# Mixer B: turning the probabilities on VectorE instead of TensorE, with the values' steps in a new order

## The chip, the cores and the metric

The kernel runs on one core of one Trainium2 chip. The metric is the device time of one execution in microseconds (us); times given for several runs are their median. One execution was also taken by the hardware profiler, and the lines quoted below are from it.

## What is computed

The program is a two-layer encoder trunk on 256 positions of width 2048, in float32. Layer 0 uses attention mixer A, layer 1 uses mixer B; each is followed by a gated MLP. The change lies in mixer B. For each of three head groups (dilations 1, 4, 16) with eight heads of 128, the reference computes

```python
logits = einsum('bnqchd,bnkchd->bnchqk', qb, kb) * scale + bias
p = exp(logits - max(logits))
o = einsum('bnchqk,bnkchd->bnqchd', p, vb)
```

and then joins the groups with weights taken from their softmax denominators. The kernel keeps the probabilities as queries on partitions by keys on columns, and the second product needs them with keys on partitions. So every block of probabilities has to be turned once. Group 0 has 256 x 256 probabilities per head; groups 1 and 2 are computed as two diagonal blocks of 128 x 128 per head.

## The kernel before, in words

**The weight stream.** Nearly all time goes into products of activations with weight matrices that are read from memory once. A weight tile of 128 x 1024 floats is loaded by SP (`raw`), and split in two parts so that TensorE can multiply it fast and still exactly: ScalarE writes the rounded part `wh` (line 128), VectorE the rest `wl = raw - wh` (line 129). TensorE then runs 12 matmuls of 512 columns on that pair, here called a **block**: for each of two rows of weights and two halves of the positions `wh` (line 153), `wl` (154) and `wh` again with the activations' low part (155). There are six `raw` buffers and three pairs of `wh` and `wl` (NHL = 3, line 23), handed out in turn (`new_hl`, line 120). So the `wh` of a block can be written only when TensorE has finished the block three places earlier. A projection (`project`, line 180) is 8 blocks, and after each block `step()` (line 90) advances one generator: the pending small work is written into the program between the blocks of the next projection.

**Mixer B** (line 917) runs in two halves of four heads (`hf`). Each half makes, for the groups 0, 1, 2, the projections k and q with the generators `k_gen` and `s_gen`, and then three projections for the values with `v_gen` (line 1002). `s_gen` leaves the probabilities of head i in tiles `pr`: for group 0 one 128 x 256 tile for each half m of the queries, for the groups 1 and 2 one 128 x 256 tile that holds both 128 x 128 blocks. It ends (lines 991 to 1000) with the factors `e`, by which the groups are joined.

**The values before.** `v_gen` first takes the projection's result out of PSUM (`evac_split`, line 689). Then, one head per step, VectorE multiplies `pr` by its factor (line 1014), TensorE transposes the blocks of 128 x 128 into PSUM (line 1016), and ScalarE and VectorE copy the result back to SBUF as `pT`: for group 0 split into a high and a low part (lines 290, 291), for the groups 1 and 2 as one plain copy by either engine in turn (lines 78 and 80). One step later TensorE multiplies `pT` with the values: for group 0 six matmuls of 256 columns (lines 307 to 309), otherwise two of 128 columns in full float32 (line 305, two records each in the trace), and the result is split into a slot `ah`, `al` that the output projection reads.

**The other way to turn.** Keys, queries and the MLP are turned without TensorE already: VectorE's transpose turns each 32 x 32 block of a tile in place (`turn_blocks`, line 332), and `place_blocks` (line 338) moves the blocks to where they belong with 16 copies on 32 partitions each. A four-letter table says which engine takes a copy; "paaa" is 4 for GpSimd (line 345) and 12 for ScalarE (line 347).

**The order.** A scheduler of the tile framework puts the instructions of each engine into a fixed queue, and each engine works its queue strictly from the front, waiting where an input is not ready. The splits of the weights are asked for with a raised priority (AHEAD = 45).

## Time and profile before

| | |
|---|---|
| three runs | 2264.11, 2264.49, 2266.11 us; median 2264.49 |
| the profiled execution | 2266.43 us, its span 2264.6 us |
| granted TensorE clock | 0.999 of full speed |
| busy share of the span | TensorE 99%, its weight loads 82%, VectorE 73%, ScalarE 67%, GpSimd 11% |
| line 1016, the transposes in question | 64 matmuls, mean 272 ns of one |
| window from 1146.60 to 1214.45 us: values of the first half | TensorE 67.74, VectorE 40.65, ScalarE 32.02, GpSimd 0.75 us busy of 67.85 |

The span is the time from the first to the last instruction. The duration of a matmul in a row is its whole passage through the engine; matmuls overlap, so what one adds to the stream is the distance from its start to the next start.

### The profile page before, as it was taken

How to read it: one execution, taken by the hardware profiler on the slowest of the kernel's cores; microseconds unless marked ns; L12 is line 12 of the kernel's file. 1: busy time of each engine (PE TensorE's matmuls, PEld its weight loads, DVE VectorE, ACT ScalarE, POOL GpSimd, SP SyncE). 2: the span in 40 equal slices, each digit the busy share in tenths (PEclk: the TensorE clock that was granted, in tenths of full speed). 3: DMA queues.
4: the chain of work that ended last, by engine and by line, in shares of the span. 5: the costliest groups of instructions: out<-in, count | busy, mean ns of one | idle time of the engine just before them, and what ended most of it. 6: DMA issues, size and time to landing. Idle time of an engine off the chain costs nothing.

```text
span 2264.6 us, 28910 instructions
## 1 busy us (share of the span) xinstructions
PE 2247.2 (99%) x10157; PEld 1859.7 (82%) x10157; DVE 1658.6 (73%) x2243; ACT 1511.0 (67%) x2344; POOL 257.7 (11%) x372
## 2 busy tenths in 40 slices
PE   9999999999999999999999999999999999999998
PEld 7788888888888888888888888888888888888886
DVE  6776687888878788856565556465888888688895
ACT  6665776777547777767755775565777754577763
POOL 2210112200001010121100100000101100001101
PEclk9999999999999999999999999999999999999999
DMA  8444557755665655666655564565656656556664
GB/s 299 156 149 150 197 196 224 223 188 190 209 205 187 201 189 188 208 218 203 192 172 178 177 193 160 183 195 187 196 192 194 204 186 212 188 191 193 218 202 135
DMA packets 126450, 437.43 MB, mean 193 GB/s; under 512 B 17264, under 2 KB 18032, under 8 KB 126304
## 3 DMA queue, kind: packets, MB, share of 16 engines
q1 hardware_dynamic: 119744, 425.64, 57.5%
q0 software_dynamic: 6128, 9.38, 1.6%
q8 instruction: 79, 1.29, 0.2%
q14 instruction: 67, 0.55, 0.1%
q10 hardware_dynamic: 432, 0.56, 0.1%
HBM read 429.20 MB, written 6.29 MB: 192 GB/s over the span
## 4 chain that ended last, share of the span: by engine, by line
PE 80%; DVE 1%; DMA 1%; ACT 1%; issue 1%; POOL 0%; POOLq 0%; DVEq 0%; ACTq 0%
PE acc L154 21%; PE acc L155 21%; PE acc L153 21%; PE acc L273 5%; PE acc L275 5%; PE acc L278 5%; DMA scr<-lnt 1%; PE ps L305 1%; DVE wl L129 1%; ACT tM L347 0%; PE ps L1016 0%; DMA raw<-in_w_down_dram 0%; ACT wh L128 0%; PE ps L308 0%; PE ps L309 0%
## 5 line engine op out<-in xcount | busy, mean ns | idle before, releaser
L129 DVE TENSOR_TENSOR wl<-raw,wh 128x1024 fp32r<-128x1024 f32 x828 | 1017.7, 1235 | 452.7 <-ACT wh L128 449.8
L128 ACT ACTIVATE wh<-raw 128x1024 fp32r<-128x1024 f32 x828 | 872.9, 1058 | 538.0 <-PE acc L155 325.8
L153 PE MATMUL acc<-wh,xh 128*128 128x512 f32 x2176 | 852.2, 392 | 0.2 <-ACT wh L164 0.2
L154 PE MATMUL acc<-wl,xh 128*128 128x512 f32 x2176 | 848.3, 390 | 3.1 <-DVE wl L129 2.9
L155 PE MATMUL acc<-wh,xh 128*128 128x512 f32 x2176 | 847.4, 389 | 0.0
L154 PEld LDWEIGHTS acc<-wl,xh 128*128 128x128 f32 x2176 | 408.7, 188 | 89.7 <-DVE wl L129 6.3
L155 PEld LDWEIGHTS acc<-wh,xh 128*128 128x128 f32 x2176 | 408.4, 188 | 84.9
L153 PEld LDWEIGHTS acc<-wh,xh 128*128 128x128 f32 x2176 | 408.9, 188 | 83.7 <-ACT wh L164 0.7
L345 POOL COPY u<-t 32x256 f32<-32x256 f32 x176 | 110.7, 629 | 1040.3 <-DVE t L455 1032.2
L273 PE MATMUL acc<-wh,ah 128*128 128x512 f32 x520 | 202.5, 389 | 1.3 <-DVE h L408 1.3
L275 PE MATMUL acc<-wh,al 128*128 128x512 f32 x520 | 202.3, 389 | 0.0
L154 PE MATMUL acc<-wl,ah 128*128 128x512 f32 x480 | 187.1, 390 | 1.0 <-DVE wl L129 1.0
L153 PE MATMUL acc<-wh,ah 128*128 128x512 f32 x480 | 187.3, 391 | 0.1
L155 PE MATMUL acc<-wh,al 128*128 128x512 f32 x480 | 186.6, 389 | 0.0
L347 ACT ACTIVATE u<-t 32x256 f32<-32x256 f32 x352 | 147.8, 420 | 13.8 <-DVE t L455 5.8
L278 PE MATMUL acc<-wl,ah 128*128 128x512 f32 x520 | 146.1, 389 | 0.0
L273 PEld LDWEIGHTS acc<-wh,ah 128*128 128x128 f32 x520 | 97.6, 188 | 22.2 <-DVE h L408 2.0
L278 PEld LDWEIGHTS acc<-wl,ah 128*128 128x128 f32 x520 | 97.6, 188 | 20.3
L275 PEld LDWEIGHTS acc<-wh,al 128*128 128x128 f32 x520 | 97.6, 188 | 20.2
L154 PEld LDWEIGHTS acc<-wl,ah 128*128 128x128 f32 x480 | 90.1, 188 | 20.1 <-DVE wl L129 1.8
L153 PEld LDWEIGHTS acc<-wh,ah 128*128 128x128 f32 x480 | 90.1, 188 | 19.0 <-DVE cu L628 0.6
L155 PEld LDWEIGHTS acc<-wh,al 128*128 128x128 f32 x480 | 90.1, 188 | 18.5
(180 smaller groups left out, 1666.4 us busy)
## 6 DMA issues: line engine op xcount, KB each, us to landing
raw<-in_w_up_dram SPq DMA_DIRECT2D x352, 512.0 KB, 4.3
raw<-in_w_down_dram SPq DMA_DIRECT2D x176, 512.0 KB, 4.8
raw<-in_w_b_dram SPq DMA_DIRECT2D x144, 512.0 KB, 4.3
raw<-in_w_bo_dram SPq DMA_DIRECT2D x48, 512.0 KB, 4.1
raw<-in_w_a_dram SPq DMA_DIRECT2D x40, 512.0 KB, 4.5
raw<-in_w_ao_dram SPq DMA_DIRECT2D x32, 512.0 KB, 3.8
raw<-in_w_a_dram SPq DMA_DIRECT2D x16, 256.0 KB, 6.5
h<-in_x_dram SPq DMA_DIRECT2D x4, 512.0 KB, 8.2
```

Of the source, the lines that this page charges most:

```text
L128: nc.scalar.activation(wh, r, AF.Copy)
L129: nc.vector.tensor_tensor(wl, r, wh.bitcast(F32), ALU.subtract)
L153: nc.tensor.matmul(accs[m], xh, wh[:, j, :], start=st, stop=False)
L154: nc.tensor.matmul(accs[m], xh, wl[:, j, :], start=False, stop=False)
L155: nc.tensor.matmul(accs[m], xl, wh[:, j, :], start=False, stop=sp)
L273: nc.tensor.matmul(acc[k], xh, wh[:, j, :], start=k in fresh, stop=False)
L275: nc.tensor.matmul(acc[k], xl, wh[:, j, :], start=False, stop=False)
L278: nc.tensor.matmul(acc[k], xh, wl[:, j, :], start=False, stop=last[k] == i and j == 1)
L305: nc.tensor.matmul(o, lh[ls], rh[rs], start=start, stop=stop)
L345: nc.gpsimd.tensor_copy(dst, src)
L347: nc.scalar.activation(dst, src, AF.Copy)
```

## The change

`v_gen` no longer uses TensorE to turn the probabilities. After the scaling, VectorE's transpose turns the 32 x 32 blocks of `pr` into a tile `tp` of 128 x 1024 (tag "stg", two buffers that the evacuated keys and queries use too), and `place_blocks(..., "paaa")` moves them into a tile `pp`, in the space of tiles that are free by then. For group 0 one `tp` holds two heads, and ScalarE and VectorE then split `pp` into `pT` as before; for the groups 1 and 2 one `tp` holds all four heads and TensorE reads `pp` directly. The work is spread over the steps by a `plan`: for group 0 eight steps (turn, place and turn, place, split, then split and multiply), for the others five (turn, place, nothing, two heads' products, two heads' products). `s_gen` only gains a third view of the same `pr` tile.

```diff
@@ -980,7 +980,7 @@
                             pr = [hpool.tile([P, NT], F32, tag=f"a{c}{sl}", name=nm("pr")) for c in "hl"]
                         else:
                             pt = hpool.tile([P, NT], F32, tag=f"ah{sl}", name=nm("pr"))
-                            pr = [pt[:, :P], pt[:, P:]]
+                            pr = [pt[:, :P], pt[:, P:], pt]
                         for m in range(2):
                             c = 4 * m + i
                             nc.scalar.activation(pr[m], lg[:, m, :W], AF.Exp, bias=nmx[:, g, c:c + 1],
@@ -1001,41 +1001,60 @@
 
                 def v_gen(g, accs, hf=hf, probs=probs, e=e):
                     v = evac_split(bp, accs, rstd, g > 0)
-                    pTs = {}
-                    yield
-                    for k in range(5):
-                        yield
-                        if k < 4:
-                            i = k
+                    parts = {}
+                    n_ = 2 if g == 0 else 4
+
+                    def turn(u):
+                        t = parts["t", u] = bp.tile([P, 2, 512], F32, tag="stg", name=nm("tp"), bufs=2)
+                        for i in range(u * n_, u * n_ + n_):
                             pr = probs[4 * g + i]
-                            t = ps_tile()
                             for m in range(2):
                                 c = 4 * m + i
                                 nc.vector.tensor_scalar(pr[m], pr[m], e[:, g, c:c + 1], None, op0=ALU.mult)
-                                for kt in range(2 if g == 0 else 1):
-                                    nc.tensor.transpose(t[:, kt * NT + m * P:kt * NT + (m + 1) * P],
-                                                        pr[m][:, kt * P:(kt + 1) * P], ident)
-                            pT = pTs[i] = pair_tile(bp, [P, 2 * NT], "pT", 2, g > 0)
-                            n = 2 * NT if g == 0 else NT
-                            split(pT[0][:, :n], pT[1] if pT[1] is None else pT[1][:, :n], t[:, :n])
-                        if k >= 1:
-                            i = k - 1
-                            j = i % 2
-                            pT = pTs.pop(i)
-                            if j == 0:
-                                o = ps_tile()
-                            for kt in range(2):
-                                vs = (allp, kt, slice(i * P, (i + 1) * P))
                                 if g == 0:
-                                    mm3(o[:, j * NT:(j + 1) * NT], v, pT, vs,
-                                        (allp, slice(kt * NT, (kt + 1) * NT)), kt == 0, kt == 1)
-                                else:
-                                    mm3(o[:, j * NT + kt * P:j * NT + (kt + 1) * P], v, pT, vs,
-                                        (allp, slice(kt * P, (kt + 1) * P)), True, True)
-                            sl = (2 * g + hf) * 4 + i
-                            slots[sl] = new_slot(sl)
-                            hi, lo = slots[sl]
-                            split(hi, lo, o[:, j * NT:(j + 1) * NT])
+                                    nc.vector.transpose(t[:, m, i % 2 * NT:i % 2 * NT + NT], pr[m])
+                            if g > 0:
+                                nc.vector.transpose(t[:, :, i * P:(i + 1) * P],
+                                                    pr[2].rearrange("p (m c) -> p m c", m=2))
+
+                    def place(u):
+                        o = bp.tile([P, 4, NT], F32, tag=("qTl", "qTh", "kTh")[g] if u == 0 else "kTl", name=nm("pp"))
+                        place_blocks(o.rearrange("p j (m t) -> p j m t", m=2), parts.pop(("t", u)), "paaa")
+                        for i in range(n_):
+                            parts[u * n_ + i] = o[:, 2 * i:2 * i + 2, :] if g == 0 else (o[:, i, :], None)
+
+                    def low(i):
+                        src = parts[i].rearrange("p a t -> p (a t)")
+                        parts[i] = pair_tile(bp, [P, 2 * NT], "pT", 2)
+                        split(*parts[i], src)
+
+                    def value(i):
+                        j = i % 2
+                        if j == 0:
+                            parts["o"] = ps_tile()
+                        o, pT = parts["o"], parts.pop(i)
+                        for kt in range(2):
+                            vs = (allp, kt, slice(i * P, (i + 1) * P))
+                            if g == 0:
+                                mm3(o[:, j * NT:(j + 1) * NT], v, pT, vs,
+                                    (allp, slice(kt * NT, (kt + 1) * NT)), kt == 0, kt == 1)
+                            else:
+                                mm3(o[:, j * NT + kt * P:j * NT + (kt + 1) * P], v, pT, vs,
+                                    (allp, slice(kt * P, (kt + 1) * P)), True, True)
+                        sl = (2 * g + hf) * 4 + i
+                        slots[sl] = new_slot(sl)
+                        split(*slots[sl], o[:, j * NT:(j + 1) * NT])
+
+                    if g == 0:
+                        plan = ((turn, 0), (place, 0, turn, 1), (place, 1), (low, 0), (low, 1, value, 0),
+                                (low, 2, value, 1), (low, 3, value, 2), (value, 3))
+                    else:
+                        plan = ((turn, 0), (place, 0), (), (value, 0, value, 1), (value, 2, value, 3))
+                    yield
+                    for fs in plan:
+                        yield
+                        for f, a in zip(fs[::2], fs[1::2]):
+                            f(a)
 
                 for g in range(3):
                     bts = biases(hf, g)
```

The instructions stand differently in three queues. The rows below are from the first half of mixer B; the second half has the same sequence. The numbers in names tell tiles apart.

ScalarE before, from the factors `e` at the end of `s_gen` on:

```order
L995 ACTIVATE e_8857<-e_8857 128x24
L128 ACTIVATE wh_10328<-raw_10324 128x1024
L290 ACTIVATE pTh_10241<-ps_10234 128x512
L128 ACTIVATE wh_10366<-raw_10325 128x1024
L290 ACTIVATE pTh_10272<-ps_10265 128x512
L290 ACTIVATE ah_10283<-ps_10276 128x256
L128 ACTIVATE wh_10396<-raw_10392 128x1024
L290 ACTIVATE pTh_10310<-ps_10303 128x512
```

Between two weight splits there stood one or two copies. ScalarE after, from the same place on:

```order
L995 ACTIVATE e_8857<-e_8857 128x24
L128 ACTIVATE wh_10326<-raw_10322 128x1024
L128 ACTIVATE wh_10346<-raw_10323 128x1024
L347 ACTIVATE pp_10263<-tp_10234 32x8x32 x12
L347 ACTIVATE pp_10305<-tp_10280 32x8x32 x9
L128 ACTIVATE wh_10381<-raw_10377 128x1024
L347 ACTIVATE pp_10305<-tp_10280 32x8x32 x3
L290 ACTIVATE pTh_10342<-pp_10263 128x512
L128 ACTIVATE wh_10411<-raw_10378 128x1024
```

Twenty-one placing copies of the two turned tiles of group 0 now stand between `wh_10346` and `wh_10381`, the splits for two blocks that follow each other on TensorE.

VectorE before, from the first scaling on:

```order
L1014 TENSOR_SCALAR pr_9349<-pr_9349,e_8857 128x256
L1014 TENSOR_SCALAR pr_9350<-pr_9350,e_8857 128x256
L1014 TENSOR_SCALAR pr_9383<-pr_9383,e_8857 128x256
L129 TENSOR_TENSOR wl_10329<-raw_10324,wh_10328 128x1024
L291 TENSOR_TENSOR pTl_10242<-ps_10234,pTh_10241 128x512
```

VectorE after, from the same place on:

```order
L1013 TENSOR_SCALAR pr_9349<-pr_9349,e_8857 128x256
L1013 TENSOR_SCALAR pr_9350<-pr_9350,e_8857 128x256
L1015 STREAM_TRANSPOSE tp_10234<-pr_9349 128x256
L1015 STREAM_TRANSPOSE tp_10234<-pr_9350 128x256
L1013 TENSOR_SCALAR pr_9383<-pr_9383,e_8857 128x256
L1013 TENSOR_SCALAR pr_9384<-pr_9384,e_8857 128x256
L1015 STREAM_TRANSPOSE tp_10234<-pr_9383 128x256
L1015 STREAM_TRANSPOSE tp_10234<-pr_9384 128x256
L129 TENSOR_TENSOR wl_10327<-raw_10322,wh_10326 128x1024
```

Four scalings and four transposes now stand ahead of the split `wl_10327`; four more of each stand between it and `wl_10347`, and between that and `wl_10382` the four transposes of group 1 and twelve of the sixteen scalings of the groups 1 and 2. In the same way the copies of group 1 and 2 follow on ScalarE in pieces of 1, 4, 7, 4, 6 and 2 between later weight splits.

TensorE before, at the first products of group 0 (rows of the weight stream are L153 to L155):

```order
L1016 MATMUL ps_10234<-ident,pr_9349 128x128 x2
L1016 MATMUL ps_10234<-ident,pr_9350 128x128 x2
L153 MATMUL acc_10177<-wh_10249,xh_8590 128x512
L154 MATMUL acc_10177<-wl_10250,xh_8590 128x512
L155 MATMUL acc_10177<-wh_10249,xh_8590 128x512
L153 MATMUL acc_10178<-wh_10249,xh_8590 128x512
L154 MATMUL acc_10178<-wl_10250,xh_8590 128x512
L155 MATMUL acc_10178<-wh_10249,xh_8590 128x512
L1016 MATMUL ps_10265<-ident,pr_9383 128x128 x2
L307 MATMUL ps_10276<-pTh_10241,vh_10171 128x256
L308 MATMUL ps_10276<-pTl_10242,vh_10171 128x256
```

TensorE after, at the same products:

```order
L155 MATMUL acc_10178<-wh_10346,xh_8760 128x512
L153 MATMUL acc_10177<-wh_10381,xh_8905 128x512
L153 MATMUL acc_10178<-wh_10381,xh_8905 128x512
L154 MATMUL acc_10177<-wl_10382,xh_8905 128x512
L307 MATMUL ps_10366<-pTh_10342,vh_10171 128x256
L155 MATMUL acc_10177<-wh_10381,xh_8905 128x512
L154 MATMUL acc_10178<-wl_10382,xh_8905 128x512
L155 MATMUL acc_10178<-wh_10381,xh_8905 128x512
L308 MATMUL ps_10366<-pTl_10343,vh_10171 128x256
L309 MATMUL ps_10366<-pTh_10342,vl_10172 128x256
L307 MATMUL ps_10366<-pTh_10342,vh_10171 128x256
```

The transposes are gone from the queue. The first products stand inside the block of `wh_10381`, four blocks later than before, and at the head of that block two matmuls on `wh_10381` stand ahead of the first on `wl_10382`, the only place in each half where the order 153, 154, 155 is broken so.

## The prediction

> **What bounds the kernel now.** I read the page first, for the engine that is never idle, then the list of waits for what stops it.

> ```profile
> span 2264.6 us, 28910 instructions
> PE 2247.2 (99%) x10157; PEld 1859.7 (82%) x10157; DVE 1658.6 (73%) x2243; ACT 1511.0 (67%) x2344; POOL 257.7 (11%) x372
> PE 80%; DVE 1%; DMA 1%; ACT 1%; issue 1%; POOL 0%; POOLq 0%; DVEq 0%; ACTq 0%
> PE acc L154 21%; PE acc L155 21%; PE acc L153 21%; PE acc L273 5%; PE acc L275 5%; PE acc L278 5%; DMA scr<-lnt 1%; PE ps L305 1%; DVE wl L129 1%; ACT tM L347 0%; PE ps L1016 0%; DMA raw<-in_w_down_dram 0%; ACT wh L128 0%; PE ps L308 0%; PE ps L309 0%
> ```

> TensorE is busy for 99% of the span, and the chain that ended last is its weight stream. The transposes of line 1016 are in that chain too. The waits of TensorE from 900 to 1480 us, which holds all of mixer B, are one row:

> ```profile
> engine line waited for: us in total, times, longest us
> PE acc L154 <- DVE wl L129: 0.5, 1, 0.5
> ```

> So in mixer B nothing stops TensorE, and whatever leaves its queue comes off the time, unless something new makes it wait. Both sides are worked out below for one half of mixer B; the halves are alike:

> ```profile
> core 0: us, PE busy (x) PEld busy (x) DVE busy (x) ACT busy (x) POOL busy (x), PEclk, DMA share, GB/s
> 1146.60:1214.45 67.85, 67.74 (x344) 56.67 (x342) 40.65 (x73) 32.02 (x50) 0.75 (x1) 1.00 0.52 168
> 1359.81:1427.68 67.87, 67.75 (x343) 56.66 (x342) 40.66 (x73) 32.02 (x50) 0.00 (x0) 1.00 0.50 164
> ```

> Each window runs from one weight matmul behind a score product to one behind the last product of the values but one. It holds 21 blocks.

> **What the transposes cost.** The row of line 1016 gives 272 ns for each of 64, but they overlap, so I take what they add to the stream.

> ```profile
> L1016 PE MATMUL ps<-ident,pr 128*128 128x128 f32 x64 | 11.2, 272 | 0.2
> 1164.43 0.39 PE L155 MATMUL acc<-wh,xh 128*128 128x512 f32 x1
> ...
> 1165.84 0.39 PE L155 MATMUL acc<-wh,xh 128*128 128x512 f32 x1
> ...
> 1189.29 0.39 PE L155 MATMUL acc<-wh,xh 128*128 128x512 f32 x1
> 1189.52 0.60 PE L305 MATMUL ps<-pT,v 128*128 128x128 f32 x4
> ...
> 1190.42 0.39 PE L155 MATMUL acc<-wh,xh 128*128 128x512 f32 x1
> 1190.65 0.39 PE L153 MATMUL acc<-wh,xh 128*128 128x512 f32 x1
> ...
> 1193.37 0.39 PE L153 MATMUL acc<-wh,xh 128*128 128x512 f32 x1
> ```

> From 1190.65 to 1193.37 are 12 weight matmuls, so one takes 0.227 us and a block 2.72. The six products of a head of group 0 lie between the line-155 matmuls at 1164.43 and 1165.84, beside three weight steps: 1.41 - 0.68 = 0.73. The four records of line 305 in the same way: 1.13 - 0.68 = 0.45. The window holds 252 weight matmuls (57.1), four heads of group 0 (2.9) and eight of the others (3.6), together 63.6 of 67.85. The rest, **4.2 us**, is 32 transposes and the small wait ahead of the first, 0.13 us each. About 0.1 is given back, since the first head's products are now cut in two by three weight matmuls. I take 4.1 per half, 8.2 in all.

> **What is added beside the stream.** Per half ScalarE gets 48 placing copies and gives up four copies from PSUM, VectorE gets 16 transposes and gives up four copies, GpSimd gets 16 copies. With 32 and 41 us busy of 68, ScalarE and VectorE have room in the mean, and GpSimd is idle. So where the new work stands decides, and I follow one stretch.

> **The wait that is added.** ScalarE now has 21 placing copies in one piece between the weight splits `wh_10346` and `wh_10381`. Behind them wait `wh_10381`, then VectorE's `wl_10382`, then TensorE. The rows for the walk:

> ```profile
> 1149.19 0.39 PE L155 MATMUL acc<-wh,xh 128*128 128x512 f32 x1
> 1149.41 0.39 PE L153 MATMUL acc<-wh,xh 128*128 128x512 f32 x1
> 1149.66 1.06 ACT L128 ACTIVATE wh<-raw 128x1024 fp32r<-128x1024 f32 x1 [0.22 <-PE acc L155]
> 1056.57 2.99 ACT L347 ACTIVATE kT<-tT 32x256 f32<-32x256 f32 x7
> L347 ACT ACTIVATE kT<-tT 32x256 f32<-32x256 f32 x48 | 19.9, 415 | 0.7
> 1081.59 1.06 ACT L128 ACTIVATE wh<-raw 128x1024 fp32r<-128x1024 f32 x1
> 1082.69 1.22 DVE L129 TENSOR_TENSOR wl<-raw,wh 128x1024 fp32r<-128x1024 f32 x1 [2.44 <-ACT wh L128]
> ```

> Up to here both orders are the same. The split at 1149.66 is `wh_10326`; it starts 0.47 us after the start of the last matmul of the block that frees its buffer. Without waits TensorE then works the blocks of `wh_10247` from 1149.41, `wh_10289` from 1152.13, `wh_10326` from 1154.85, `wh_10346` from 1157.57 and `wh_10381` from 1160.29. The buffer for `wh_10346` comes free with the last matmul of the block 10247 (start 1151.90), so that split runs from 1152.37 to 1153.43. Then come the copies. Seven like them took 2.99 us, each 0.415 long, so they follow each other every 0.43 us: 21 take 9.0. They end at 1162.45, `wh_10381` at 1163.5 and, 0.04 later started and 1.22 long, `wl_10382` at 1164.75.

> TensorE would want `wl_10382` two matmuls into its block, at 1160.75. It gets it at about 1164.8 and has waited **4.1 us**. Its next instruction, a product with `pTh_10342`, stands behind three more placing copies (1.3 us) and that split of 128x512 (0.6) on ScalarE, so it can start at 1163.5 + 1.3 + 0.6 = 1165.4, some **0.4** after its turn.

> **Does VectorE come into it?** Its rows:

> ```profile
> 1150.55 0.88 DVE L1014 TENSOR_SCALAR pr<-pr,e 128x256 f32<-128x256 f32 x3
> 1160.30 1.65 DVE L1014 TENSOR_SCALAR pr<-pr,e 128x128 f32<-128x128 f32 x8
> 1151.34 1.22 DVE L129 TENSOR_TENSOR wl<-raw,wh 128x1024 fp32r<-128x1024 f32 x1
> L335 DVE STREAM_TRANSPOSE tT<-stg 128x512 f32<-128x512 f32 x24 | 16.9, 706 | 6.1 <-ACT stg L686 6.1
> L291 DVE TENSOR_TENSOR al<-ps,ah 128x256 fp32r<-128x256 f32 x40 | 16.6, 416 | 0.0
> L291 DVE TENSOR_TENSOR pTl<-ps,pTh 128x512 fp32r<-128x512 f32 x24 | 16.4, 683 | 0.0
> 1056.58 2.70 POOL L345 COPY kT<-tT 32x256 f32<-32x256 f32 x4 [22.12 <-DVE tT L335]
> ```

> A transpose of 128x256 is not in the trace. It lies between half of the 706 ns of 128x512 and the whole; line 291 loses 267 ns from 512 to 256 columns, so I take 0.44, with 0.36 from start to start. From 1150.55 four scalings (0.27 apart) and four transposes end at 1153.1, before ScalarE is free for the copies at 1153.45: no delay. At 0.7 us each they would end at 1154.2, and all of the chain moves by 0.8. The split `wl_10327` then starts at 1153.05 and ends at 1154.3, in time for 1155.1. The next eight end at 1156.8 and `wl_10347` at 1157.9, some 0.1 behind TensorE's 1157.8; that is inside the 4.1, which counts from the undisturbed stream. The transposes of group 1 need `tp`'s buffer, freed by the twelfth copy at 1158.6 and by GpSimd's four (2.7 us, done by 1156). Four of them and nine scalings take 3.3, to 1161.9, before `wh_10381` is ready. So ScalarE sets the wait.

> **Groups 1 and 2.** Here the copies stand in pieces of 1, 4, 7, 4, 6 and 2 between the splits of the weights, and ScalarE is behind after the wait.

> ```profile
> L290 ACT ACTIVATE pTh<-ps 128x512 fp32r<-128x512 f32 x24 | 14.3, 594 | 5.9 <-PE ps L868 3.5 <-PE ps L1016 2.0
> L290 ACT ACTIVATE ah<-ps 128x256 fp32r<-128x256 f32 x40 | 15.0, 374 | 0.2
> L294 ACT ACTIVATE v<-acc,rstd 128x512 f32<-128x512 f32 x8 | 5.4, 680 | 3.7 <-PE acc L155 3.7
> ```

> From 1163.5 on, ahead of `wh_10592`, the split for the second block after the one of `wh_10543`, ScalarE has 25 copies (10.7), six weight splits (6.4), four `pTh` (2.4), four `ah` (1.5) and two evacuations of the values (1.4): 22.4 us, so `wh_10592` runs from 1185.9 and its `wl` ends at 1188.2. TensorE has from 1164.8 ten matmuls and the 0.4, four heads' products (3.0), six blocks (16.3), and then one product of group 1 and a first matmul (0.7): it wants that `wl` at 1187.5. I take **0.5** between 0, if the copies' small overlaps and waits come out so, and 1.0. SP's queue is unchanged, and six `raw` buffers give a load some 16 us of lead; so loads cost nothing.

> **The sum.** Per half: -4.1 + 4.1 + 0.4 + 0.5 = +0.9; in all **+1.8 us**. Against the profiled execution, 2266.43 us with 2264.6 of span, that is 2268.2; the median of the runs is 1.9 lower, so I forecast 2264.5 + 1.8 = **2266.3 us**. Bounds of the unknown: the transposes up to +0.8 per half, groups 1 and 2 from -0.5 to +0.5, so 2265.3 to 2268.9; I allow 1.5 below for the walk, 2263.8. All of it is within 0.2% (4.5 us, about what a measurement of this kernel can tell from no change).

> [...]

> **Rivals.** *The stream does not wait: faster.* Then the 8.2 us come off whole: 2256.3. For it speaks that the keys and queries are placed in the same way today without a wait. Against it: there ScalarE had one split of weights after six or seven copies, and here none for 21. To be in time `wl_10382` must end at 1160.7, so the copies at 1158.4, in 5.0 us; that needs 0.24 us a copy where the 48 of the row above show 0.415. Halfway houses would need the trace's order to differ from the queue's. Chance 0.12.

> *The wait slows the clock: slower.* TensorE stands from about 1160.4 to 1163.5 with nothing, has two matmuls and stands again until 1164.8, once per half. No gap of that length is in this trace. The longest of TensorE's waits in the whole run is the last number of this row:

> ```profile
> PE acc L154 <- DVE wl L129: 3.9, 6, 1.5
> ```

> It is 1.5 us, and the granted clock is 1.00 in both windows, so a drop is neither shown nor excluded. If the clock were halved for as long again as the gap (4.1 us), each half would lose 2.05 more: 2266.3 + 4.1 = 2270.4; for twice as long, 2274.5. It decides if the first gap, 3.1 us and twice the longest that this trace has without a drop, is enough. Chance 0.18. [...]

> *Longer waits of the plain kind,* as from a queue that stays behind through groups 1 and 2, by over 1.5 us per half: 2269 to 2272, chance 0.08. *That the transposes stay on TensorE* is excluded by the queue, which no longer holds them.

> **How the numbers follow.** Forecast 0.62, no wait 0.12, slow clock 0.18, longer waits 0.08. Same: 0.62; faster by over 0.2%: 0.12; slower by over 0.2%: 0.26. The range must leave out no more than 0.2: it leaves out the case without a wait (0.12) and the longer form of the slow clock (about 0.06), and reaches from 2261.5, half of the way to the first, to 2272.0.

> **What would show it.** Right: line 1016 gone; TensorE with two waits in each half on `wh` (near 3 us) and `wl` (1.3) in the block 10381, near 8 us in all, and one of about 0.5 at `wl_10593`; 96 placing copies at 0.415; the stretch of both windows longer by some 0.9 us. Wrong: a granted clock below 0.95 just behind those waits, weight matmuls more than 0.227 apart there, or no wait on lines 128 and 129 at all. The forecast falls if ScalarE's copies run faster beside GpSimd's than the rows show, or if the order of a queue is not kept.

## The result, and the profile after

| | before | after |
|---|---|---|
| median of six runs each | 2265.45 us (2264.11 to 2269.23) | 2273.45 us (2271.52 to 2277.99) |
| ratio, with its 95% interval | | 1.0036 (1.0023 to 1.0049) |
| profiled execution, its span | 2266.43 us, 2264.6 us | 2274.62 us, 2272.8 us |
| granted TensorE clock | 0.999 | 0.997 |

The changed kernel is 8.0 us slower. The forecast was 2266.3 and its range ended at 2272.0, so both missed. The first lines of the page of after:

```profile
span 2272.8 us, 28932 instructions
PE 2247.1 (99%) x10093; PEld 1855.4 (82%) x10093; DVE 1667.7 (73%) x2267; ACT 1548.7 (68%) x2432; POOL 274.1 (12%) x404
```

TensorE has lost its 64 transposes and is busy as long as before (2247.2): what is left takes longer. The waits of TensorE from 900 to 1480 us, where before had one of 0.5:

```profile
engine line waited for: us in total, times, longest us
PE acc L153 <- ACT wh L128: 5.6, 2, 2.8
PE acc L154 <- DVE wl L129: 1.0, 2, 0.5
PE ps L305 <- DVE al L291: 1.0, 2, 0.5
```

To see what mixer B itself loses, I cut both traces at the same instructions: the first score product of the first half, that of the second half, and the last row of line 381, which stands behind mixer B in the same code (in the rows of that line the last start, behind "to"). Before, then after, the timeline and the rows of the line:

```profile
1044.85 0.28 PE L307 MATMUL ps<-kTh,qTh 128*128 128x256 f32 x1
...
1258.07 0.28 PE L307 MATMUL ps<-kTh,qTh 128*128 128x256 f32 x1
```

```profile
L381 PE MATMUL ps<-ident,h x24: 270/272/275, 271.7 to 1551.0; 128*128 128x128 f32 x24
```

```profile
1048.28 0.28 PE L307 MATMUL ps<-kTh,qTh 128*128 128x256 f32 x1
...
1264.70 0.28 PE L307 MATMUL ps<-kTh,qTh 128*128 128x256 f32 x1
```

```profile
L381 PE MATMUL ps<-ident,h x24: 270/272/273, 271.5 to 1560.2; 128*128 128x128 f32 x24
```

First half: 213.22 before, 216.42 after. Second half to the end of mixer B: 292.93 and 295.50. Together 506.15 and 511.92, **5.8 us more**. This sum, "mixer B" from here on, is taken in the same way from every profile below. Of the 8.2 us between the two spans a further 3.4 had been lost before the first cut, in code that the change does not touch, and 1.0 came back behind the last. Runs 13 to 16 deal with that.

Where the 5.8 us come from is seen at the block of `wh_10381`. The timeline of TensorE and then of ScalarE, after, columns start, duration, instruction, idle time before:

```profile
1163.82 0.39 PE L155 MATMUL acc<-wh,xh 128*128 128x512 f32 x1
1166.99 0.73 PE L153 MATMUL acc<-wh,xh 128*128 128x512 f32 x2 [2.79 <-ACT wh L128]
1168.25 0.59 PE L154 MATMUL acc<-wl,xh 128*128 128x512 f32 x1 [0.53 <-DVE wl L129]
1168.93 0.58 PE L307 MATMUL ps<-pTh,vh 128*128 128x256 f32 x1
1169.31 0.63 PE L155 MATMUL acc<-wh,xh 128*128 128x512 f32 x1
1169.73 0.63 PE L154 MATMUL acc<-wl,xh 128*128 128x512 f32 x1
1170.16 0.63 PE L155 MATMUL acc<-wh,xh 128*128 128x512 f32 x1
```

```profile
1156.89 8.97 ACT L347 ACTIVATE pp<-tp 32x256 f32<-32x256 f32 x21
1165.88 1.06 ACT L128 ACTIVATE wh<-raw 128x1024 fp32r<-128x1024 f32 x1
```

The 21 copies take 8.97 us in one piece, and the split behind them comes late, as the walk of the prediction had it. New is what follows: weight matmuls start 0.43 us apart instead of 0.227. The same place in stretches (the third number from the end is PEclk, the granted clock):

```profile
1168.00:1168.50 0.50, 0.25 (x1) 0.19 (x1) 0.38 (x2) 0.48 (x2) 0.00 (x0) 1.00 0.00 0
1168.50:1169.00 0.50, 0.41 (x2) 0.07 (x1) 0.35 (x2) 0.50 (x2) 0.00 (x0) 0.51 0.00 0
1169.00:1171.50 2.50, 2.50 (x9) 2.21 (x10) 2.50 (x4) 2.29 (x3) 0.00 (x0) 0.50 0.64 210
1171.50:1172.00 0.50, 0.50 (x3) 0.48 (x3) 0.18 (x1) 0.11 (x1) 0.00 (x0) 0.58 0.00 0
1172.00:1174.00 2.00, 2.00 (x12) 1.70 (x11) 1.69 (x3) 1.44 (x3) 0.00 (x0) 1.00 0.72 236
```

The clock is at 0.50 from 1168.5 to 1171.9, 3.4 us, and in the second half from 1383.55 to 1386.96. The same happened in the MLP of layer 0, at 0.50 from 400.51 to 403.92, behind a stop of 2.90 us there.

### The profile page after: what moved, and what is told of

The parts are those of the page before. It is cut to its first block, busy times and chain, and to the rows that moved or that the text cites. A ratio compares the mean times of both kernels' runs of the same rounds, so it can differ in the third digit from the quotient of the medians.

```text
span 2272.8 us, 28932 instructions
## 1 busy us (share of the span) xinstructions
PE 2247.1 (99%) x10093; PEld 1855.4 (82%) x10093; DVE 1667.7 (73%) x2267; ACT 1548.7 (68%) x2432; POOL 274.1 (12%) x404
## 4 chain that ended last, share of the span: by engine, by line
PE 78%; ACT 2%; DVE 1%; DMA 1%; issue 1%; POOL 0%; POOLq 0%; DVEq 0%; ACTq 0%
PE acc L155 21%; PE acc L154 21%; PE acc L153 21%; PE acc L273 5%; PE acc L278 5%; PE acc L275 5%; ACT pp L347 1%; DMA scr<-lnt 1%; DVE wl L129 1%; ACT wh L128 1%; PE ps L305 1%; ACT tM L347 0%; DMA raw<-in_w_down_dram 0%; PE ps L307 0%; PE ps L309 0%
## 5 line engine op out<-in xcount | busy, mean ns | idle before, releaser
L129 DVE TENSOR_TENSOR wl<-raw,wh 128x1024 fp32r<-128x1024 f32 x828 | 1016.3, 1234 | 442.4 <-ACT wh L128 439.9
L128 ACT ACTIVATE wh<-raw 128x1024 fp32r<-128x1024 f32 x828 | 872.7, 1058 | 491.2 <-PE acc L155 302.3
L153 PE MATMUL acc<-wh,xh 128*128 128x512 f32 x2176 | 852.0, 392 | 5.8 <-ACT wh L128 5.6
L154 PE MATMUL acc<-wl,xh 128*128 128x512 f32 x2176 | 850.2, 391 | 6.0 <-DVE wl L129 4.9
L155 PE MATMUL acc<-wh,xh 128*128 128x512 f32 x2176 | 849.3, 390 | 0.0
L154 PEld LDWEIGHTS acc<-wl,xh 128*128 128x128 f32 x2176 | 409.5, 188 | 95.3 <-DVE wl L129 10.8
L153 PEld LDWEIGHTS acc<-wh,xh 128*128 128x128 f32 x2176 | 409.1, 188 | 89.9 <-ACT wh L128 6.4
L155 PEld LDWEIGHTS acc<-wh,xh 128*128 128x128 f32 x2176 | 409.4, 188 | 84.8
L345 POOL COPY u<-t 32x256 f32<-32x256 f32 x176 | 110.7, 629 | 1040.8 <-DVE t L455 1032.7
L273 PE MATMUL acc<-wh,ah 128*128 128x512 f32 x520 | 202.5, 389 | 0.3 <-DVE h L408 0.3
L275 PE MATMUL acc<-wh,al 128*128 128x512 f32 x520 | 202.3, 389 | 0.0
L154 PE MATMUL acc<-wl,ah 128*128 128x512 f32 x480 | 187.1, 390 | 1.0 <-DVE wl L129 1.0
L153 PE MATMUL acc<-wh,ah 128*128 128x512 f32 x480 | 187.2, 390 | 0.0
L155 PE MATMUL acc<-wh,al 128*128 128x512 f32 x480 | 186.8, 390 | 0.0
L347 ACT ACTIVATE u<-t 32x256 f32<-32x256 f32 x352 | 147.7, 420 | 13.7 <-DVE t L455 5.8
L278 PE MATMUL acc<-wl,ah 128*128 128x512 f32 x520 | 146.1, 389 | 0.0
L273 PEld LDWEIGHTS acc<-wh,ah 128*128 128x128 f32 x520 | 97.6, 188 | 21.2 <-DVE h L408 1.0
L278 PEld LDWEIGHTS acc<-wl,ah 128*128 128x128 f32 x520 | 97.6, 188 | 20.3
L275 PEld LDWEIGHTS acc<-wh,al 128*128 128x128 f32 x520 | 97.6, 188 | 20.2
L154 PEld LDWEIGHTS acc<-wl,ah 128*128 128x128 f32 x480 | 90.1, 188 | 20.1 <-DVE wl L129 1.9
L153 PEld LDWEIGHTS acc<-wh,ah 128*128 128x128 f32 x480 | 90.1, 188 | 19.1 <-DVE cu L628 0.7
L155 PEld LDWEIGHTS acc<-wh,al 128*128 128x128 f32 x480 | 90.1, 188 | 18.5
```

What stands on the lines that cost most here:

```text
L128: nc.scalar.activation(wh, r, AF.Copy)
L129: nc.vector.tensor_tensor(wl, r, wh.bitcast(F32), ALU.subtract)
L153: nc.tensor.matmul(accs[m], xh, wh[:, j, :], start=st, stop=False)
L154: nc.tensor.matmul(accs[m], xh, wl[:, j, :], start=False, stop=False)
L155: nc.tensor.matmul(accs[m], xl, wh[:, j, :], start=False, stop=sp)
L273: nc.tensor.matmul(acc[k], xh, wh[:, j, :], start=k in fresh, stop=False)
```

## Experiments

**Theory A:** the one piece of 21 copies on ScalarE stops TensorE, and the stop costs a second time, since the clock halves behind it. **Rivals:** smaller pieces only move the stop, and over 1 us of waiting stays (B); VectorE's turning or the paired products of groups 1 and 2 cost the time (C); GpSimd becomes the bound (D); the unchanged MLP explains it (E); the half clock has another cause, or costs nothing since ScalarE is late anyway (in runs 2, 8 and 9). Each ratio is taken against runs of the kernel before from the same series (their medians lie between 2265.01 and 2265.74 us); differences to the changed kernel go across series.

**Run 1, placing in two steps.** `place` takes 8 of the 16 blocks at a time:

```diff
- plan = ((turn, 0), (place, 0, turn, 1), (place, 1), (low, 0), (low, 1, value, 0),
-         (low, 2, value, 1), (low, 3, value, 2), (value, 3))
+ plan = ((turn, 0), (place, 0, turn, 1), (place, 1), (place, 2, low, 0),
+         (place, 3, low, 1, value, 0), (low, 2, value, 1), (low, 3, value, 2), (value, 3))
...
- plan = ((turn, 0), (place, 0), (), (value, 0, value, 1), (value, 2, value, 3))
+ plan = ((turn, 0), (place, 0), (place, 1), (value, 0, value, 1), (value, 2, value, 3))
```

> The changed kernel, but the placing copies of a turned tile are issued in two steps of 8 instead of one of 16 (place takes a half), so that ScalarE has 12 copies ahead of the split for the block at which TensorE stopped, instead of 21, and 6 and 6 behind it. Nothing is left out. Theory A (the piece of 21 copies makes TensorE stop, the stop of 2.8 us is followed by 3.4 us at half clock; all the rest of the change is a gain): 12 copies take 5.2 us, so that split ends near the time it is wanted, the wait on wh and the stretch at clock 0.50 go in both halves; of the 6.8 us per half that the stop and the clock take by the trace (2.9 for wh, 0.6 for wl, 1.6 by the clock, and small ones behind it) some 5 to 6 come back: 10 to 12 us, to about 2262. Theory B (a stop stays, the copies only move it: ScalarE is behind all the same): over 1 us of waiting on wh or wl stays per half and the time stays above 2268. Theory C (what costs is VectorE's part or the pairs of products in groups 1 and 2): no change within 2 us of 2273.

Measured: 2269.38 us, 1.0022 (1.0013 to 1.0031) of before; mixer B 510.4. The waits from 1040 to 1480 us, and the clock in and behind the first stop of each half:

```profile
PE ps L307 <- ACT pTh L290: 3.9, 2, 1.9
PE ps L305 <- DVE al L291: 3.7, 2, 2.0
PE ps L307 <- DVE al L291: 0.5, 1, 0.5
```

```profile
1160.00:1163.00 3.00, 1.06 (x5) 0.60 (x4) 2.47 (x9) 2.94 (x6) 0.00 (x0) 1.00 0.48 161
1163.00:1166.50 3.50, 3.50 (x12) 2.97 (x11) 2.95 (x8) 3.39 (x9) 1.35 (x4) 0.52 0.29 94
...
1376.00:1379.00 3.00, 1.08 (x6) 0.76 (x5) 2.47 (x9) 2.94 (x6) 0.00 (x0) 1.00 0.46 162
1379.00:1382.50 3.50, 3.50 (x20) 2.96 (x19) 2.94 (x8) 3.39 (x10) 1.56 (x4) 1.00 0.32 102
```

The wait on `wh` is gone, but others took its place: ScalarE works almost without a break from 1152.9 to 1189 (busy for 7.83 of the 8.00 us from 1160 to 1168), so whatever stands behind its copies is late, first `pTh`, then `al`. Theory A is missed by 7 us. B came true in its time and in kind, though what stayed is not a wait on `wh` or `wl`, as it had it. The two halves are a comparison by themselves: the same stop of 1.9 us, behind one the clock is halved (12 matmul records in 3.5 us), behind the other not (20). Against before the first half loses 2.6 us and the second 1.8.

**Run 2, 12 more matmuls for TensorE**, to fill the stop, ahead of it.

```diff
+ if g == 0 and fs[-2:] == (place, 1):
+     t = ps_tile()
+     with tc.high_priority(offset=0):
+         for _ in range(12):
+             nc.tensor.matmul(t, v[0][:, 0, :P], v[0][:, 0, :], start=True, stop=True)
```

> The changed kernel with 12 additional matmuls of 512 columns per half on TensorE (2.7 us), on the values' tile, into a free PSUM bank that nobody reads, inside the third block from the one at which TensorE stopped (two blocks ahead of it). Nothing is left out. The wait is for ScalarE's copies and ends at the same time, so these matmuls fill the stop instead of adding to it. Theory A (the stop costs twice, once as a wait and once by the clock behind it): the granted clock stays at 1.00 through both windows, the idle time in front of the block shrinks to 0.5 us or less, and the time falls by about 1.6 us per half, 3 us in all, to 2270. Rival (the half clock comes from something else, as the load of the other engines or the transfers): the clock falls to 0.50 all the same and the time is not below 2273.

Measured: 2274.0 us, 1.0043 (1.003 to 1.0055); mixer B 514.2. Missed: the scheduler put the first product of group 0 ahead of the block, so TensorE stood before that for 2.3 us, and the clock fell behind it in both halves (0.997 granted over the whole execution). It does not tell A from its rival, since the stop was not filled. **Run 8** added 10 more:

```diff
+ if g == 0 and fs[:2] == (low, 0):
+     t = ps_tile()
+     with tc.high_priority(offset=0):
+         for _ in range(10):
+             nc.tensor.matmul(t, v[0][:, 0, :P], v[0][:, 0, :], start=True, stop=True)
```

> As the run with 12 additional matmuls, and 10 more on the next block, all ahead of the first product of group 0, where TensorE then stood for 2.34 us and the clock fell behind it. Nothing is left out. 22 matmuls are 5.0 us of additional work per half. Theory A (a stop of over 2 us costs a further 1.7 us by the clock): no stop over 1 us at group 0, the clock at 1.00 through both windows, and the time 3.4 us below that of 12 matmuls: 2270.5, although TensorE has 4.5 us more to do. Rival: the clock falls all the same, or the time is 2274 or more.

Measured: 2277.44 us, 1.0054 (1.0041 to 1.0066); mixer B 519.2. Missed again: TensorE now stood 2.4 us before the second head's product, which waited for `al`. The clock fell in one half only, the second:

```profile
1168.70:1171.50 2.80, 0.41 (x3) 0.02 (x1) 2.04 (x4) 2.73 (x7) 2.21 (x4) 1.00 0.34 126
1171.50:1175.00 3.50, 3.50 (x18) 3.05 (x19) 1.22 (x2) 3.44 (x7) 0.78 (x1) 1.00 0.43 150
...
1388.50:1391.50 3.00, 0.61 (x4) 0.19 (x3) 2.21 (x5) 2.93 (x7) 2.33 (x4) 1.00 0.34 126
1391.50:1392.00 0.50, 0.50 (x5) 0.50 (x6) 0.41 (x1) 0.49 (x2) 0.50 (x1) 1.00 0.07 25
1392.00:1395.50 3.50, 3.50 (x11) 2.82 (x11) 1.32 (x2) 3.42 (x8) 0.16 (x1) 0.51 0.40 146
```

More work for TensorE ahead of a late engine is no cure: the waits behind ScalarE moved on and stayed. And here the rival has a point: against before the first half, without half clock, loses 6.7 us and the second, with it, 6.4. In the first TensorE stood 1.3 us once more, for `al` of a later product, and in the second it did not: there the slow stretch cost nothing that a wait would not have cost.

**Run 3, before without its transposes.** The product takes the probabilities as they are:

```diff
- nc.tensor.transpose(t[:, kt * NT + m * P:kt * NT + (m + 1) * P], pr[m][:, kt * P:(kt + 1) * P], ident)
...
- n = 2 * NT if g == 0 else NT
- split(pT[0][:, :n], pT[1] if pT[1] is None else pT[1][:, :n], t[:, :n])
+ if g == 0:
+     for m in range(2):
+         c = slice(m * NT, (m + 1) * NT)
+         split(pT[0][:, c], pT[1][:, c], pr[m])
+ else:
+     split(pT[0][:, :NT], None, pr[2])
```

> The kernel before with its transposes left out: the probabilities go into the second product as they are, not turned, so that part of the computation is changed. Copies, products and their order stay. This prices what the change can win at most. By the working of the prediction (0.13 us for each of 64): 8.4 us below before, 2257.0. By the distances between starts in the trace of before (what follows a transpose, added up, 3.3 us per half): 6.7 us below, 2258.7. Were they hidden beside the weight stream: within 2 us of before.

Measured: 2257.44 us, 0.9966 (0.9954 to 0.9979), 7.6 us below before; mixer B 498.5, also 7.6 below. So the transposes cost 0.12 us each on average, and 3.8 us per half is the most that the change could win.

**Run 4, groups 1 and 2 alone** turned by VectorE, group 0 by TensorE (`v_old` is `v_gen` of before):

```diff
- start(v_gen(g, project(w_b, 6 * g + 4 + hf, hT, kgs)))
+ start((v_old if g == 0 else v_gen)(g, project(w_b, 6 * g + 4 + hf, hT, kgs)))
```

> Group 0 as before the change (TensorE turns), groups 1 and 2 as after it (VectorE turns, 24 copies of ScalarE per half in pieces of 8, 4, 4, 4 and 4). Nothing is left out. Theory A (the loss is in group 0's piece of 21 copies alone): no stop over 1 us and no stretch at half clock; 16 of 32 transposes per half gone, 1.7 to 2.1 us, less about 1.0 per half for the pairs of products that wait for each other: 1.5 to 2.5 us below before, about 2263. Theory C (groups 1 and 2 lose as well): at or above before, 2265 to 2268.

Measured: 2262.55 us, 0.9989 (0.998 to 0.9997); mixer B 502.9, 3.3 below before, with no wait of TensorE in it at all. Half of the transposes are worth 3.8 in both halves together by run 3, if all cost the same, so VectorE's turning and the pairs of groups 1 and 2 cost 0.3 us per half by themselves, and C falls. In the changed kernel groups 1 and 2 lose 1.0 us per half against run 3. The 0.7 beyond run 4 is ScalarE's lateness, carried on from group 0: one product of line 305 per half waits for `al` there, its start 0.64 us later than the usual step would put it, and none does in run 4.

**Run 5, one letter:** GpSimd places 8 of 16 blocks instead of 4.

```diff
- place_blocks(o.rearrange("p j (m t) -> p j m t", m=2), parts.pop(("t", u)), "paaa")
+ place_blocks(o.rearrange("p j (m t) -> p j m t", m=2), parts.pop(("t", u)), "ppaa")
```

> The changed kernel with one letter of the table changed: ppaa, so that GpSimd places 8 of the 16 blocks of a turned tile and ScalarE 8 instead of 12. Nothing is left out. The first run with smaller pieces showed that ScalarE is busy without a break from the first placing copy on to the products of group 1, so that a stop only moved to the next thing that waited for it. Theory A (ScalarE's queue is what TensorE waits for): 8 copies ahead of the split instead of 21, 32 per half instead of 48; the split comes in time, the first pTh stands behind 8 further copies and is 1 to 1.5 us late, groups 1 and 2 lose 1 us: some 2.5 us per half instead of 7; no stretch at half clock; 2262. Theory D (GpSimd's copies of 0.65 us or VectorE beside them become the bound): waits of 2 us or more for pTh or pp on GpSimd's side, the time above 2268.

Measured: 2262.13 us, 0.9986 (0.9977 to 0.9995); mixer B 503.1, as theory A had it, and the clock stays at full speed (0.999 granted over the whole execution, as before). The longest of its waits of TensorE from 1040 to 1480 us:

```profile
PE ps L307 <- ACT pTh L290: 2.3, 2, 1.1
```

**Run 12** has `"pppa"`:

> The changed kernel with the table pppa: GpSimd places 12 of 16 blocks, ScalarE 4, 16 per half. Nothing is left out. A dose after paaa (48 copies of ScalarE per half, mixer B 511.9) and ppaa (32, 503.1). If only ScalarE's queue counted, mixer B would fall further, to 501 or 502. Theory D (GpSimd, at 0.65 us a copy 7.8 us a tile, becomes the one that is waited for): the second tile of group 0 is placed 15.6 us after the first is ready, some 1 us late for the third head; mixer B at 502.5 to 504, with a wait of TensorE that goes back to GpSimd.

Its longest waits in the same stretch, and from its timeline a row of GpSimd and one of ScalarE:

```profile
PE ps L307 <- DVE al L291: 5.9, 2, 2.9
PE ps L307 <- ACT pTh L290: 1.5, 2, 0.8
```

```profile
1152.19 15.79 POOL L345 COPY pp<-tp 32x256 f32<-32x256 f32 x24 [4.74 <-DVE tp L1015]
...
1168.02 0.63 ACT L290 ACTIVATE pTh<-pp 128x512 fp32r<-128x512 f32 x1 [2.73 <-POOL pp L345]
```

It measured 2272.42 us, 1.0024 (1.0015 to 1.0034), mixer B 513.7. Of three doses the middle one is best: with 48 copies per half ScalarE is late, with 16 GpSimd is, whose 24 copies take 15.8 us; its part in the expectation (D) was right, its size not, because the wait for GpSimd stands in ScalarE's queue and holds up what is behind it. A stop of 2.9 us came of it, and the clock fell to 0.50 again, from 1168.76 on for 3.41 us and from 1383.80 on for 6.83.

**Run 6, three edits:** two steps, `"ppaa"`, and a PSUM tile per head in groups 1 and 2 (`if j == 0 or g > 0: parts["o"] = ps_tile()`).

> Three edits together: placing in two steps of 8 blocks, the table ppaa, and a PSUM tile of its own for each head of the groups 1 and 2, so that the second product of a pair does not wait for the result of the first to be read. Nothing is left out. Theory A: no stop over 0.5 us in mixer B, clock 1.00; all of what the kernel without turning won comes off but for the cut of the group-0 products: 7 us below before, 2258. Theory D (GpSimd as the bound): 2262 or more, with a wait for pTh. If the pairs of products cost for another reason than the shared PSUM tile, 1 us per half stays: 2260.

Measured: 2262.03 us, 0.9988 (0.9979 to 0.9996); mixer B 502.9, no better than run 5, and 4 us above what theory A had. No stop at `pTh`, but one of 1.3 us per half in group 0, for `al` of the head that shares the PSUM tile:

```profile
PE ps L307 <- DVE al L291: 2.6, 2, 1.3
```

**Run 7, the MLP of layer 0.** There VectorE copies six table lines (line 911) into two buffers and waits for their stores; a weight split stands behind the copy. The edit lets lines 2 to 5 use quarters whose store is older:

```diff
- ln = lnt[:, b % 2]
+ ln = lnt[:, b % 2] if b < 2 else lnt[:, b // 4, 256 * (b % 2):]
```

> The changed kernel, and in the MLP of layer 0 the table lines b = 2 to 5 are laid out so that a copy on line 911 waits for one store that is long done instead of the last but one. Mixer B stays as in the changed kernel; nothing is left out. In the profiles so far TensorE stood there for 1.46 us (before), 2.90 (after), 0, 3.46, 0.71 and 2.58, in code that is the same in all of them. Theory E (that stop changes from run to run and hides 2 us or more of the result): the stop goes, the time falls by 2 to 5 us to 2269 to 2271, and the runs lie closer together. If the stop has little to do with it, 2273.

Measured: 2271.34 us, 1.0026 (1.0016 to 1.0035), 2.1 below the changed kernel; the stop is gone. **Run 11** is the same edit on the kernel before:

> The kernel before with the table layout in the MLP of layer 0 alone; nothing is left out. If the stop there is one and the same thing in both kernels, 1.5 to 3 us below before, 2262 to 2263.5, and the difference of the changed kernel with this layout (2271.3) to it is what mixer B loses in their profiles, near 8 us. If the stop belongs to the change: within 0.5 us of before.

Measured: 2264.72 us, 0.9994 (0.9986 to 1.0003), no difference that can be told, where 1.5 to 3 us were expected if the stop is the same thing in both. Without that stop in either kernel the change still costs 2271.34 - 2264.72 = 6.6 us (7.2 by the ratios). So E explains little. In run 7 the clock stayed at half for 6.8 us per half instead of 3.4 (0.996 granted over the whole execution, against 0.997), and mixer B took 514.3, though its code is that of the changed kernel.

**Run 9, TensorE kept at work during the stop.** Three small products per half read what the copies have just written:

```diff
+ for q in range(4):
+     place_blocks(ov, tv, "paaa", range(4 * q, 4 * q + 4))
+     if g == 0 and u == 1 and q < 3:
+         w = ps_tile()
+         with tc.high_priority(offset=0):
+             nc.tensor.matmul(w[:, :NT], ident, ov[:, :, :, 32 * q:32 * q + 32], start=True, stop=True)
```

> The changed kernel with three additional products of 256 columns in full float32 per half, each reading what four of the placing copies of the second tile have just written, into a free PSUM bank that nobody reads. The order of ScalarE, VectorE, GpSimd and SP is the same to the instruction, and so is that of TensorE but for these three, which stand in the block ahead of the one at which TensorE stopped. They become ready at about 1163.3, 1164.6 and 1165.9 in the times of the changed kernel, so that the stop of 2.8 us is cut in pieces of under 1.6 us with work between them, while ScalarE's queue and the end of the wait stay. Nothing is left out. Theory A (the long stop halves the clock): no stretch at half clock, and mixer B (the two halves together, 511.9 us in the profile of the changed kernel, 514.3 in that of the run with the other table layout, 506.2 before) takes 508 to 509.5; the time is about 3.5 us below 2273.4. Rival (the half clock has nothing to do with the length of the stop, or costs nothing since ScalarE is late anyway): mixer B at 512 or more.

Measured: 2269.96 us, 1.0016 (1.0008 to 1.0025), 3.5 below the changed kernel; mixer B 510.0, 0.5 above what was expected. TensorE's timeline there, and the clock:

```profile
1158.84 0.50 PE L154 MATMUL acc<-wl,xh 128*128 128x512 f32 x1
1160.82 0.67 PE L1028 MATMUL ps<-pp,ident 128*128 128x256 f32 x2 [1.48 <-POOL pp L345]
...
1162.11 0.67 PE L1028 MATMUL ps<-pp,ident 128*128 128x256 f32 x2 [0.16 <-issue]
...
1163.40 0.67 PE L1028 MATMUL ps<-pp,ident 128*128 128x256 f32 x2 [0.15 <-issue]
...
1165.76 0.44 PE L154 MATMUL acc<-wl,xh 128*128 128x512 f32 x1
1166.38 0.39 PE L307 MATMUL ps<-pTh,vh 128*128 128x256 f32 x1 [0.18 <-ACT pTh L290]
```

```profile
1158.00:1162.00 4.00, 2.44 (x9) 1.21 (x7) 4.00 (x14) 3.87 (x10) 2.30 (x4) 1.00 0.41 133
1162.00:1166.00 4.00, 3.74 (x15) 2.67 (x15) 2.51 (x6) 3.85 (x9) 1.64 (x4) 1.00 0.01 2
1166.00:1170.00 4.00, 3.82 (x21) 3.14 (x21) 3.85 (x7) 4.00 (x7) 0.00 (x0) 1.00 0.44 155
```

ScalarE's queue and its lateness are those of the changed kernel, and TensorE has more to do, yet the clock stays at 1.00 in both halves and the time falls as expected. That shows the second half of theory A: the half clock came from the stop and cost 2 to 4 us (mixer B 510.0 against 511.9 to 514.3). The other 3.8 us that mixer B loses against before are still there.

**Run 10, the version to keep:** run 6, with a PSUM tile per head in group 0 too (`o, pT = ps_tile(), parts.pop(i)`), and the edit of run 7.

> Placing in two steps, table ppaa, a PSUM tile of its own for every head (group 0 too), and the table layout in the MLP of layer 0. Nothing is left out. In the profile of the run with pieces, ppaa and own tiles for the groups 1 and 2, what was left in mixer B was a wait of 1.3 us per half of a product of group 0 for the result of the head that shares its PSUM tile, and 0.4 for wl. If that is so, mixer B takes 500 to 501 us (before 506.2, without turning 498.5), the stop in the MLP is gone, and the time is 2256 to 2258. If another wait of ScalarE's queue takes its place, mixer B stays at 502.5 or more and the time above 2259.

Measured: 2259.25 us, 0.9968 (0.9955 to 0.998), 6.5 below before, and faster than either kernel; mixer B 499.5, 1.0 above that without any turning. What TensorE still waits for there, two times 0.2 us:

```profile
PE acc L154 <- DVE wl L129: 0.4, 2, 0.2
```

The time lies 1.3 us above what was expected, mixer B 0.5 below. Of the 6.5 us, run 11 puts 1.0 on the edit of run 7 alone, within its noise; mixer B by itself gains 6.7.

**Runs 13 to 16, the two kernels again**, for more profiles.

> The changed kernel once more, for a second profile of it. If the length of the slow stretches is chance (they begin 3.41 us apart or at multiples of it, so where the stop falls decides), the two halves take anything from 511.9 to 514.3 us, with slow stretches of 3.41 or 6.83 us at the same two places; if it belongs to the program, 511.9 again. The stop in the MLP of layer 0: 2.90 again if it belongs to the program, anything from 0 to 3.6 if it is chance.

> The changed kernel a third time, with the same question: two halves of 511.9 us again, or anything up to 514.3; a stop of 2.90 us in the MLP of layer 0 again, or anything from 0 to 3.6.

> The kernel before once more, for a second profile of it: the two halves of mixer B 506.2 as in the first, no slow stretch there. The stop in the MLP of layer 0: 1.46 again if it belongs to the program, anything from 0 to 3.6 if it is chance.

> The kernel before a third time, with the same question: two halves of 506.2 us; a stop of 1.46 us in the MLP of layer 0 again, or anything from 0 to 3.6.

| | time of the profiled execution | mixer B | slow clock, half 1 and 2 | stop in the MLP of layer 0 |
|---|---|---|---|---|
| before | 2266.43 | 506.2 | none | 1.5 |
| run 15 | 2263.19 | 506.1 | none | 0 |
| run 16 | 2269.40 | 506.2 | none | 2.6, then 3.4 us slow |
| after | 2274.62 | 511.9 | 3.4, 3.4 us | 2.9, then 3.4 us slow |
| run 13 | 2270.49 | 513.1 | 6.8, 3.4 us | 0 |
| run 14 | 2271.47 | 513.2 | 6.8, 3.4 us | 1.4 |

Mixer B before is the same to 0.1 us; after, it takes 5.8 to 7.0 us more (8.2 in run 7), by the length of the slow stretch. A single execution does not tell the kernels apart: run 16 is within 1.1 us of run 13. The stop in the MLP is chance in both kernels: it ends when a store has landed, for which the copy of line 911 waits 3.73 us in the profile of before and 5.18 in that of after (why that comes earlier or later was not tried), and the rest of the 8.0 us lies within what it and the interval of the ratio (5 to 11 us) allow.

## Why the prediction was wrong

- **Bound (right):** TensorE's stream is the bound (99% busy in both), and before it had one wait of 0.5 us from 900 to 1480 us.
- **Transposes (right in kind, 0.3 too much):** 3.8 us per half instead of 4.1 (run 3).
- **The wait behind 21 copies (right):** 4.1 and 0.4 us were forecast up to the product with `pTh_10342`. By starts, less the usual 0.227, it was 2.94 for `wh`, 0.81 up to the first matmul on `wl` and 0.45 up to the product, 4.2 in all, the last already at half clock in part.
- **VectorE (right):** its 128x256 transposes took 0.40 to 0.44 us, and `wl_10347` was 0.2 to 0.3 late, where 0.1 was forecast and counted as nothing. Beyond that it set no wait of its own.
- **Groups 1 and 2 (right in size within its bounds, wrong in place):** 1.0 us per half, the upper bound instead of 0.5. Of it 0.64 is not a wait for `wl_10593`, but a product of line 305 that waited for `al`, since two heads share a PSUM tile and ScalarE was late in reading it; 0.3 is there without that wait too (run 4).
- **The failed step: the sum has no term for the clock, on the ground that "a drop is neither shown nor excluded" (chance 0.18).** The stop halved the clock each time, for 3.4 or 6.8 us, in all three profiles of the changed kernel and in run 7, with weight matmuls 0.43 us apart behind it, which is the sign of being wrong that the prediction names. This was the rival, with the right mechanism; its point of decision, a first gap of 3.1 us, was met but for 0.2 (2.94 by starts). The walk that I held for likely gave that gap, and nothing in the trace spoke against a drop behind it, so the 0.18 was too low. The rival's price was put at 2 to 4 us per half. Half by half against run 9 it is 1.3 and 0.7 for stretches of 3.4 us (after), and 2.0 and 2.4 for 6.8 us (run 7), since part of a slow stretch falls into waits.
- **What that leaves.** In the first profile mixer B lost 5.8 us where 1.8 was forecast. About half of the 4.0 between them is the clock (2.0). The rest is there in run 9 at full clock, where mixer B loses 3.8: 0.6 less won, 1.0 more in groups 1 and 2 and, by difference, 0.4 around the stop, where small delays that the sum had no term for (`wl_10347` above all) outweigh the shorter wait. It is the clock that took the time out of the range: run 9, at 2269.96, lies inside it.

## What to carry to other kernels

An engine with room in the mean can still be the bound where its work stands in one piece (here ScalarE, busy for 68% of the span): count what lies between two instructions that a busier engine waits for, and shift some of it to an idle engine until neither is late (one letter gave back 11 us here). A stop of a TensorE-bound stream can cost twice, as a wait and as a stretch at half clock of 3.4 or 6.8 us: here one of two stops of 1.9 us (run 1) did, and both of 2.8 (after). The second part is less, or nothing (run 8), where later waits take it up. Where a wait is removed, look in the same queue for the next instruction that somebody waits for.

## What the runs showed of the hardware

**A transpose of line 1016 costs less than its record:** 272 ns in the row, 0.12 us of the stream (7.6 us for 64, run 3).
